# A decoder block on one core: the first norm's conditioning worked in by two weight chunks at every second output tile

## The chip, the cores and the metric

The kernel runs on one core of a Trainium2 chip. A core has five engines that work side by side, each in the order in which its own instructions stand: TensorE for matmuls (PE in the profile, PEld for its weight loads), VectorE (DVE), ScalarE (ACT), GpSimd (POOL) and SyncE (SP), which here issues the loads of weights. Sixteen DMA engines move data between the HBM and the on-chip memory. The metric is the device time of one execution in microseconds.

## The reference

The reference is one step of a decoder block (one layer, width 2048) over 288 tokens: 256 of a prompt and 8 samples of 4 tokens. The two request groups share all weights. Cut to what matters here:

```
mod = silu(c) @ w_ada + b_ada                  # 2048 -> 6 parts of 2048
sh1, sc1, g1, sh2, sc2, g2 = split(mod, 6)     # one row per sequence: 1 + 8
h    = rmsnorm(x, norm1) * (1 + sc1) + sh1     # the first norm, conditioned
proj = h @ w_in                                # pooling, gate, x/B/C, dt columns
...                                            # pooling mixer, Mamba-2 scan
x = x + g1 * (mix @ w_out)
h2 = rmsnorm(x, norm2) * (1 + sc2) + sh2
x = x + g2 * (conv_ffn(h2))                    # up, causal conv, SiLU, down
y = rmsnorm(x, norm_f)
```

"Conditioning of the first norm" is the making of `sh1` and `sc1`: 9 rows of `silu(c)` (padded to 32) times a weight matrix of 2048 × 4096. Only when they are there for some 128 rows of the hidden width can these rows of `h` be made, and only then can the projection `h @ w_in` use them.

## The kernel before, in words

Activations lie transposed: the hidden width on the 128 partitions, in 16 blocks called K tiles, and the 288 tokens along the free dimension. A projection's output tile is 128 output columns by 288 tokens. Operands of the projections are split into a high and a low part, so that each K tile of an output tile takes three matmuls: high by high, high by low, low by high (`mm3`, L221 to L223).

All weights come as chunks of 128 × 1024 words of 4 bytes (512 KB) through one set of eight buffers (`raw`), loaded by `load` (L209) on SP's queue. A chunk of the projection is then split: ScalarE casts it to the high part (L215) and VectorE subtracts to get the low part (L216); high and low have two buffers each, so a new chunk is split when the one before the last has been used up. The raw buffer is free after the subtraction. A chunk of the conditioning's weights isn't split: TensorE reads it straight from its raw buffer as float32 (`ada_mm`, L250), four narrow matmuls side by side in four column strips of the array, and the buffer is free when they are done.

The input projection begins before the conditioning of all rows is there. The K tiles are cut into six groups of 1, 1, 2, 4, 4 and 4 (`KGROUPS`). For each group in turn, `xbc_units` goes over 28 output tiles (`ET`), multiplies the group's K tiles into each, and adds the result to sums in the on-chip memory: by ScalarE's copies for the first group, by VectorE's adds (L536) for the others. While it does so, the conditioning of the next group is worked in between the output tiles: `ada_group_units` is a generator that loads one chunk, yields, and at its next step multiplies that chunk and loads another. The loop calls it once after each output tile, from tile `NX[gi]` on:

```
for i, m in enumerate(xbc_units(gi)):
    if not last:
        if i >= NX[gi]:
            next(nxt, None)
        if i == ET - 4:
            drain(nxt)
            modulate(...)
```

A step of this kind between two output tiles is called a visit here. The second group's conditioning has 4 chunks, the third's 8 (of 16 narrow passes on TensorE each, over 128 columns), and the fourth's, fifth's and sixth's 16 each (8 passes over 256 columns). A group's projection weights come in chunks of 8 output tiles for the first two groups, of 4 for the third, of 2 for the others. When the last chunk is in, the result is copied out of PSUM, transposed on TensorE and added to the bias; then `modulate` makes the group's rows of `h` (in halves again, `h1h` and `h1l`, L348 and L349).

The program text is not yet the order on the engines. A planner of the kernel language puts each engine's instructions, SP's loads too, in order when the kernel is built: it takes the earliest in the text among those that are ready by its own estimate of times, and gives out buffers as by that estimate they come free. Where it reckons a chunk late, it lets other matmuls go first; so a visit can be cut in two, or two visits can meet.

After the projection, `ada_part_units` makes the other four parts of the conditioning in the same manner; it handles two K tiles to a visit already (`AY`). Then follow the mixer, the output projection, and the feed-forward part with the gate, value and down matmuls, which fill the time from about 500 us on.

Of the kernel before, what the change touches and what calls it, by code (L numbers as in the profile page):

```python
# [19 lines left out]
KT = D // P  # L20
# [19 lines left out]
SPLIT1, SPLIT2 = 2, 2  # L40
YK = 2
NX = (10, 1, 1, 1, 1)
AY = 2

RA1, RA2, RB1, RB2, RB3 = 0.5, 0.4, 1.0, 1.0, 1.0
# [42 lines left out]
def _halves(nk):  # L88
    return [(0, 8), (8, nk - 8)]
# [40 lines left out]
def kernel(ctx: ExitStack, tc, ins, outs):  # L130
# [9 lines left out]
    def aux(name):  # L140
        return px.tile([P, 512], F32, tag="aux", name=name)
# [18 lines left out]
    ada = kp.tile([P, 6, KT, NC9], F32, name="ada")  # L160
# [8 lines left out]
    def warm_pe(n, rhs=None):  # L169

        for _ in range(n):
            nc.tensor.matmul(wps[:, :P], ones, ones if rhs is None else rhs, start=True, stop=True)
# [33 lines left out]
    def load(key):  # L206
        off, cols = S.items[key]
        t = wp[0].tile([P, RAWC], F32, tag="raw", name="raw_" + "_".join(map(str, key)))
        nc.sync.dma_start(t[:, :cols], wflat[off:off + P * cols].rearrange("(p n) -> p n", p=P))  # L209
        return t  # L210

    def split(raw, a, n, name):
        hi = wp[0].tile([P, RAWC], F32R, tag="whi", name="whi_" + name)
        lo = wp[0].tile([P, RAWC], F32R, tag="wlo", name="wlo_" + name)
        nc.scalar.copy(hi[:, :n], raw[:, a:a + n])  # L215
        nc.vector.tensor_tensor(lo[:, :n], raw[:, a:a + n], hi[:, :n].bitcast(F32), ALU.subtract)  # L216
        return hi, lo

    def mm3(ps, whi, wlo, c, bh, bl, first, last, n=P):
        w = slice(c * n, c * n + n)  # L220
        nc.tensor.matmul(ps, whi[:, w], bh, start=first, stop=False)  # L221
        nc.tensor.matmul(ps, whi[:, w], bl, start=False, stop=False)  # L222
        nc.tensor.matmul(ps, wlo[:, w], bh, start=False, stop=last)  # L223
# [23 lines left out]
    def ada_mm(ps, raw, k, c0, nb, js):  # L247
        for j in js:
            c = c0 + (j - js[0]) * nb
            nc.tensor.matmul(ps[32 * j:32 * j + 32, :nb], sc_c[:, k, :], raw[:, c:c + nb],  # L250
                             start=(k == 0), stop=(k == KT - 1), tile_position=(0, 32 * j))

    def ada_sb(ps, nb, name, r=P):
        asb = kp.tile([P, 512], F32, tag="asb", name="asb_" + name)
        nc.scalar.copy(asb[0:r, :nb], ps[0:r, :nb])
        return asb

    def ada_tr(asb, nb, name, r=P):
        pt = aux("adat_" + name)
        for i in range(nb // P):  # L260
            nc.tensor.transpose(pt[:, i * r:(i + 1) * r], asb[0:r, i * P:(i + 1) * P], ident[0:r, 0:r])
        return pt

    def ada_scale(which, part, norm, k0, gk):
        nc.vector.scalar_tensor_tensor(
            out=amul[:, which, k0:k0 + gk, :], in0=ada[:, part, k0:k0 + gk, :], scalar=1.0,
            in1=norm[:, k0:k0 + gk].unsqueeze(2).to_broadcast([P, gk, NC9]),
            op0=ALU.add, op1=ALU.mult)

    def ada_group_units(gi):  # L270

        k0, gk = KGROUPS[gi]
        nj = min(2 * gk, 4)
        nb = 2 * gk * P // nj
        per = RAWC // (nj * nb)
        ps = pa.tile([P, 512], F32, tag="ada", name=f"adag{gi}")
        for q in range(KT // per):
            raw = load(("ada", gi, q))
            yield
            if gk == 1:  # L280

                for kk in range(0, per, 2):
                    k = q * per + kk
                    for j in range(4):
                        nc.tensor.matmul(ps[32 * j:32 * j + 32, :nb], sc_c[:, k + j // 2, :],
                                         raw[:, kk * 256 + j * P:kk * 256 + j * P + P],
                                         start=(k == 0), stop=(k == KT - 2), tile_position=(0, 32 * j))
                if gi == 0 and q < WU[3]:
                    warm_pe(WU[2], raw[:, 0:P])
                continue  # L290
            for kk in range(per):
                ada_mm(ps, raw, q * per + kk, kk * nj * nb, nb, range(nj))
        r = 32 * nj
        if gk == 1:
            asb = ada_sb(ps, nb, f"g{gi}")
            pt = aux(f"adat_g{gi}")
            nc.tensor.matmul(pt[:, :r], asb[:, :nb], early[:, K_S2:K_S2 + r], start=True, stop=True)
            if gi == 0:
                warm_pe(WU[4], asb[:, 0:P])
        else:  # L300
            pt = ada_tr(ada_sb(ps, nb, f"g{gi}", r), nb, f"g{gi}", r)
        for i in range(nb // P):

            o = ada[:, 0:2, k0:k0 + gk, :].rearrange("p a (b i) c -> p a b i c", b=nj // 2)[:, :, :, i, :]
            b = bada[:, 0:2, k0:k0 + gk].rearrange("p a (b i) -> p a b i", b=nj // 2)[:, :, :, i]
            src = pt[:, i * r:(i + 1) * r].rearrange("p (a b c) -> p a b c", a=2, b=nj // 2)[:, :, :, 0:NC9]
            nc.vector.tensor_tensor(o, src, b.unsqueeze(3).to_broadcast([P, 2, nj // 2, NC9]), ALU.add)
        ada_scale(0, 1, early[:, V_N1:V_N1 + KT], k0, gk)

    def ada_part_units(part, ay=1):  # L310
        ps = pa.tile([P, 512], F32, tag="ada", name=f"adap{part}")
        for k in range(KT):
            raws = [load(("adap", part, k, h)) for h in range(2)]
            for h in range(2):
                ada_mm(ps, raws[h], k, 0, 512, range(2 * h, 2 * h + 2))
            if k % ay == ay - 1:
                yield
        asb = ada_sb(ps, 512, f"p{part}")
        yield
        pt = ada_tr(asb, 512, f"p{part}")  # L320
        for i in range(4):
            o = ada[:, part].rearrange("p (j i) c -> p j i c", j=4)[:, :, i, :]
            b = bada[:, part].rearrange("p (j i) -> p j i", j=4)[:, :, i]
            src = pt[:, i * P:(i + 1) * P].rearrange("p (j c) -> p j c", j=4)[:, :, 0:NC9]
            nc.vector.tensor_tensor(o, src, b.unsqueeze(2).to_broadcast([P, 4, NC9]), ALU.add)
        if part == 4:
            ada_scale(1, 4, vec[:, V_N2:V_N2 + KT], 0, KT)
        yield
# [54 lines left out]
    def xav(k0, gk):  # L383
        return xa[k0 // 4][:, k0 % 4:k0 % 4 + gk, :]
# [154 lines left out]
    def drain(gen):  # L539
        for _ in gen:  # L540
            pass
# [260 lines left out]
    def chain(*gens):  # L802
        for gn in gens:
            yield from gn

    adas = chain(*(ada_part_units(p, AY) for p in (2, 3, 4)))
    drain(ada_group_units(0))
    modulate(xav(0, KGROUPS[0][1]), rstd1p, 0, 0, 0, KGROUPS[0][1], "g0")
    conv0 = conv_group(0)
# [35 lines left out]
    def pull(gn, rate):  # L845

        credit[id(gn)] = credit.get(id(gn), 0.0) + rate
        while credit[id(gn)] >= 1:
            credit[id(gn)] -= 1
            next(gn, None)  # L850

    for gi in range(len(KGROUPS)):
        last = gi + 1 == len(KGROUPS)
        if last:
            hi, lo = split(load(("dt",)), 0, KT * NH, "dt")
            ps = pm.tile([P, 512], F32, tag="mm", name="mm_dt")
            for k in range(KT):
                mm3(ps[0:NH, :N], hi, lo, k, xhi[0][k], xlo[0][k], k == 0, k == KT - 1, NH)
            dt_stage(ps)
        else:  # L860
            if gi == 1:
                nc.sync.dma_start(vec, ins["vec"])
            if gi == 4:
                late_loads()
            nxt = ada_group_units(gi + 1)
            k0, gk = KGROUPS[gi + 1]
        for i, m in enumerate(xbc_units(gi)):
            if not last:
                if i >= NX[gi]:
                    next(nxt, None)  # L870
                if i == ET - 4:
                    drain(nxt)
                    modulate(xav(k0, gk), rstd1, 0, 0, k0, gk, f"g{gi + 1}")
            else:
                pull(back, 0.5 if m < 20 else RB1) if m >= 9 else None
                pull(adas, RA1 / AY)

# [3 lines left out]
    for m in list(range(4 + 3 * ZEARLY, 16)) + ULATE:  # L881
        for _ in uz_units(m):
            n += 1
            for gn in late.values():
                pull(gn, 0.5)
            pull(adas, RA2 / AY)
            pull(back, RB2 if n <= zlast else RB3)
# [3 lines left out]
        if m < 4:  # L891
            late[m] = pool_units(m)
            next(late[m])
    pull(adas, TA / AY)
    for h, (_, n) in enumerate(_halves(KT)):
# [69 lines left out]
    for m in range(16):  # L965
# [9 lines left out]
        squares(m, "a")  # L975
        pull(adas, (1 + (m >= 14 - ADA_OUT)) / AY)
        if m == 13:
# [300 lines left out]
```

## Time and profile before

| | |
|---|---|
| median of 3 runs | 1402.48 us (1401.91 to 1403.09) |
| the profiled execution | 1403.24 us, of which the span of the profile is 1401.5 us |
| TensorE busy | 99% of the span |
| VectorE, ScalarE, GpSimd busy | 59%, 41%, 20% |
| read from HBM | 309.71 MB, 228 GB/s over the span |
| granted clock of TensorE, mean | 0.997 |

The profile shows one execution. Busy times are of instructions; on TensorE the matmuls are pipelined, so that several are in flight at once and their shown durations (some 0.3 us) overlap; the distance between starts tells the rate. In the timeline a line is a start in us from the span's begin, a duration in us, the engine, the line of the kernel, the operation, what it writes and reads, and how many instructions the line stands for; in brackets stands the idle time before it and what ended it. A float32 matmul of the conditioning is shown as two passes. The names: `raw_ada` is a chunk of the conditioning's weights, `adag` its sums, `raw_xbc`, `whi_xbc` and `wlo_xbc` a chunk of the projection's and its two parts, `xbc` the projection's sums, `cvp` and `cvs` where they are added up.

### The profile page before, as it was taken

How to read it: one execution, taken by the hardware profiler on the slowest of the kernel's cores; microseconds unless marked ns; L12 is line 12 of the kernel's file. 1: busy time of each engine (PE TensorE's matmuls, PEld its weight loads, DVE VectorE, ACT ScalarE, POOL GpSimd, SP SyncE). 2: the span in 40 equal slices, each digit the busy share in tenths (PEclk: the TensorE clock that was granted, in tenths of full speed). 3: DMA queues.
4: the chain of work that ended last, by engine and by line, in shares of the span. 5: the costliest groups of instructions: out<-in, count | busy, mean ns of one | idle time of the engine just before them, and what ended most of it. 6: DMA issues, size and time to landing. Idle time of an engine off the chain costs nothing.

```text
span 1401.5 us, 26531 instructions
## 1 busy us (share of the span) xinstructions
PE 1383.4 (99%) x10589; PEld 1260.6 (90%) x10589; DVE 829.3 (59%) x1429; ACT 578.4 (41%) x941; POOL 276.7 (20%) x490
## 2 busy tenths in 40 slices
PE   8999999998999999999999999999999999999998
PEld 6677887776668898989999999999999999999998
DVE  3775667867555436844666445666665466666553
ACT  5322324365573333533443333434443344444443
POOL 0000003554332212311211000212220011122121
PEclk9999999999999999999999999999999999999999
DMA  8889886867779886688655555655555555555531
GB/s 335 320 316 321 293 286 232 331 252 254 290 259 358 311 327 245 208 277 289 231 191 177 161 169 179 206 188 187 177 181 170 178 194 188 188 193 197 181 117 68
DMA packets 97195, 323.14 MB, mean 231 GB/s; under 512 B 10736, under 2 KB 19888, under 8 KB 97072
## 3 DMA queue, kind: packets, MB, share of 16 engines
q1 hardware_dynamic: 93168, 310.57, 63.1%
q0 software_dynamic: 3184, 9.69, 2.0%
q8 instruction: 83, 1.36, 0.4%
q10 hardware_dynamic: 720, 1.19, 0.2%
q14 instruction: 40, 0.33, 0.1%
HBM read 309.71 MB, written 10.39 MB: 228 GB/s over the span
## 4 chain that ended last, share of the span: by engine, by line
PE 70%; DVE 1%; issue 0%; ACT 0%; POOL 0%; DVEq 0%; POOLq 0%; ACTq 0%
PE mm_down L223 7%; PE mm_down L221 7%; PE mm_down L222 7%; PE mm_gate L223 6%; PE mm_gate L221 6%; PE mm_val L222 6%; PE mm_gate L222 6%; PE mm_val L223 6%; PE mm_val L221 6%; PE mm_out L221 2%; PE mm_out L222 2%; PE mm_out L223 2%; PE adap L250 2%; PE mm_up L221 1%; PE mm_up L222 1%; PE mm_up L223 1%
## 5 line engine op out<-in xcount | busy, mean ns | idle before, releaser
L221 PE MATMUL mm_down<-ah,whi_down 128*128 128x288 f32 x688 | 203.7, 296 | 0.0
L223 PE MATMUL mm_down<-ah,wlo_down 128*128 128x288 f32 x688 | 203.5, 296 | 0.0
L222 PE MATMUL mm_down<-al,whi_down 128*128 128x288 f32 x688 | 203.3, 295 | 0.0
L223 PE MATMUL mm_gate<-h2h,wlo_gate 128*128 128x288 f32 x640 | 190.2, 297 | 0.0
L221 PE MATMUL mm_gate<-h2h,whi_gate 128*128 128x288 f32 x640 | 189.8, 297 | 0.0
L222 PE MATMUL mm_gate<-h2l,whi_gate 128*128 128x288 f32 x640 | 189.3, 296 | 0.0
L222 PE MATMUL mm_val<-h2l,whi_val 128*128 128x288 f32 x640 | 188.8, 295 | 0.0
L223 PE MATMUL mm_val<-h2h,wlo_val 128*128 128x288 f32 x640 | 188.5, 294 | 0.0
L221 PE MATMUL mm_val<-h2h,whi_val 128*128 128x288 f32 x640 | 188.0, 294 | 0.0
L216 DVE TENSOR_TENSOR wlo_gate<-raw_gate,whi_gate 128x1024 fp32r<-128x1024 f32 x80 | 98.0, 1225 | 141.1 <-ACT whi_gate L215 141.0
L216 DVE TENSOR_TENSOR wlo_down<-raw_down,whi_down 128x1024 fp32r<-128x1024 f32 x96 | 108.1, 1126 | 115.6 <-ACT whi_down L215 114.7
L215 ACT CAST whi_down<-raw_down 128x1024 fp32r<-128x1024 f32 x96 | 92.2, 961 | 168.6 <-PE mm_down L222 121.9
L215 ACT CAST whi_gate<-raw_gate 128x1024 fp32r<-128x1024 f32 x80 | 83.9, 1050 | 169.2 <-PE mm_gate L222 73.2
L221 PE MATMUL xbc<-h1h,whi_xbc 128*128 128x288 f32 x448 | 139.2, 313 | 1.5 <-ACT h1h L348 1.3
L215 ACT CAST whi_val<-raw_val 128x1024 fp32r<-128x1024 f32 x80 | 84.1, 1051 | 127.3 <-issue 102.4
L222 PE MATMUL xbc<-h1l,whi_xbc 128*128 128x288 f32 x448 | 132.1, 296 | 0.0
L223 PE MATMUL xbc<-h1h,wlo_xbc 128*128 128x288 f32 x448 | 130.5, 298 | 0.9 <-DVE wlo_xbc L216 0.9
L222 PEld LDWEIGHTS mm_down<-al,whi_down 128*128 128x128 f32 x688 | 129.7, 189 | 0.0
L223 PEld LDWEIGHTS mm_down<-ah,wlo_down 128*128 128x128 f32 x688 | 129.6, 188 | 0.0
L221 PEld LDWEIGHTS mm_down<-ah,whi_down 128*128 128x128 f32 x688 | 129.6, 188 | 0.0
L221 PEld LDWEIGHTS mm_gate<-h2h,whi_gate 128*128 128x128 f32 x640 | 120.5, 188 | 5.0 <-ACT ah L1031 4.2
L222 PEld LDWEIGHTS mm_gate<-h2l,whi_gate 128*128 128x128 f32 x640 | 120.7, 189 | 0.0
(341 smaller groups left out, 3100.8 us busy)
## 6 DMA issues: line engine op xcount, KB each, us to landing
raw_adap<-wflat SPq DMA_DIRECT2D x128, 512.0 KB, 5.1
raw_gate<-wflat SPq DMA_DIRECT2D x80, 512.0 KB, 3.6
raw_val<-wflat SPq DMA_DIRECT2D x80, 512.0 KB, 3.5
raw_ada<-wflat SPq DMA_DIRECT2D x64, 512.0 KB, 5.3
raw_xbc<-wflat SPq DMA_DIRECT2D x55, 512.0 KB, 5.8
raw_down<-wflat SPq DMA_DIRECT2D x48, 512.0 KB, 3.5
raw_out<-wflat SPq DMA_DIRECT2D x32, 512.0 KB, 6.5
raw_down<-wflat SPq DMA_DIRECT2D x32, 384.0 KB, 3.0
```

Source lines behind the costliest of these rows:

```text
L215: nc.scalar.copy(hi[:, :n], raw[:, a:a + n])
L216: nc.vector.tensor_tensor(lo[:, :n], raw[:, a:a + n], hi[:, :n].bitcast(F32), ALU.subtract)
L221: nc.tensor.matmul(ps, whi[:, w], bh, start=first, stop=False)
L222: nc.tensor.matmul(ps, whi[:, w], bl, start=False, stop=False)
L223: nc.tensor.matmul(ps, wlo[:, w], bh, start=False, stop=last)
L250: nc.tensor.matmul(ps[32 * j:32 * j + 32, :nb], sc_c[:, k, :], raw[:, c:c + nb], start=(k == 0), stop=(k == KT - 1), tile_position=(0, 32 ...
```

## The change

From the third K group on, the generator loads two chunks at a step and multiplies two at its next; the loop calls it at every second output tile instead of at every one. For the first two groups (`gk == 1`) all stays as it is. The number of chunks, their matmuls and their order among themselves are the same. For the third group the last chunk is multiplied at the visit after tile 9, for the later groups after tile 17, as before; the rest that `drain` would take at tile `ET - 4` is empty in both.

```diff
+AG = 2
 AY = 2
...
         ps = pa.tile([P, 512], F32, tag="ada", name=f"adag{gi}")
-        for q in range(KT // per):
-            raw = load(("ada", gi, q))
+        at = 1 if gk == 1 else AG
+        for q0 in range(0, KT // per, at):
+            raws = [load(("ada", gi, q)) for q in range(q0, q0 + at)]
             yield
-            if gk == 1:
+            for q, raw in zip(range(q0, q0 + at), raws):
+                if gk > 1:
+                    for kk in range(per):
+                        ada_mm(ps, raw, q * per + kk, kk * nj * nb, nb, range(nj))
+                    continue
                 for kk in range(0, per, 2):
...
-                continue
-            for kk in range(per):
-                ada_mm(ps, raw, q * per + kk, kk * nj * nb, nb, range(nj))
...
         for i, m in enumerate(xbc_units(gi)):
             if not last:
-                if i >= NX[gi]:
+                if i >= NX[gi] and (gk == 1 or (i - NX[gi]) % AG == 0):
                     next(nxt, None)
```

## The prediction

> **What bounds the kernel now.** I read the page first (busy shares, slices), then the table of waits, then windows of the stage that the change touches, then the timeline of single visits. The page and the waits of TensorE:
>
> ```profile
> PE 1383.4 (99%) x10589; PEld 1260.6 (90%) x10589; DVE 829.3 (59%) x1429; ACT 578.4 (41%) x941; POOL 276.7 (20%) x490
> ...
> PE   8999999998999999999999999999999999999998
> ...
> PEclk9999999999999999999999999999999999999999
> ...
> PE mm_uz L223 <- DVE wlo_uz L216: 3.0, 1, 3.0
> ...
> PE xbc L221 <- ACT h1h L348: 1.3, 1, 1.3
> ...
> PE xbc L223 <- DVE wlo_xbc L216: 0.9, 3, 0.5
> ```
>
> TensorE is occupied for 99% of the span, at the full granted clock in every slice, and its longest wait in the whole run is 3.0 us. In the stage in question, some 37 to 193 us, it waits for next to nothing: the two xbc rows. So a microsecond less of TensorE work there is a microsecond off the end, unless something else becomes late. What could become late are the weights; the windows say how near that is (columns: busy us of each engine and instructions, granted clock, share of the DMA engines, GB/s):
>
> ```profile
> 10.00:16.00 6.00, 5.70 (x59) 3.92 (x59) 1.99 (x3) 0.70 (x2) 0.00 (x0) 1.00 1.03 420
> ...
> 49.00:87.00 38.00, 37.83 (x294) 26.17 (x295) 27.57 (x83) 8.38 (x11) 0.60 (x2) 1.00 0.89 324
> 107.00:136.00 29.00, 29.00 (x253) 21.78 (x251) 13.60 (x32) 6.61 (x7) 0.00 (x0) 1.00 0.92 311
> 157.00:193.00 36.00, 36.00 (x312) 27.06 (x310) 17.20 (x39) 7.64 (x8) 0.00 (x0) 1.00 0.94 325
> ```
>
> TensorE is full in all of them, but the DMA engines are 89 to 94% busy too: a second resource lies close behind the first. Where the queue is long (10 to 16 us) they move 420 GB/s.
>
> **The price of a visit.** A visit is a switch of TensorE from the projection's matmuls to the conditioning's narrow ones and back. The timeline of TensorE around a visit with one chunk (x8: four matmuls, each shown as two passes) and around one in which two chunks happen to meet (x16):
>
> ```profile
> 111.95 0.29 PE L223 MATMUL xbc<-h1h,wlo_xbc 128*128 128x288 f32 x1
> 112.17 0.64 PE L250 MATMUL adag<-raw_ada,sc_c 128*32 128x256 f32 x8
> 112.74 0.40 PE L221 MATMUL xbc<-h1h,whi_xbc 128*128 128x288 f32 x1
> 112.98 0.30 PE L222 MATMUL xbc<-h1l,whi_xbc 128*128 128x288 f32 x1
> 113.11 0.29 PE L223 MATMUL xbc<-h1h,wlo_xbc 128*128 128x288 f32 x1
> ...
> 82.46 0.30 PE L223 MATMUL xbc<-h1h,wlo_xbc 128*128 128x288 f32 x1
> 82.70 1.07 PE L250 MATMUL adag<-raw_ada,sc_c 128*32 128x256 f32 x16
> 83.70 0.40 PE L221 MATMUL xbc<-h1h,whi_xbc 128*128 128x288 f32 x1
> 83.93 0.30 PE L222 MATMUL xbc<-h1l,whi_xbc 128*128 128x288 f32 x1
> ```
>
> Matmuls are pipelined, so starts are what counts. Projection matmuls start 0.13 us apart (112.98 to 113.11). From the last one before a visit to the second one after it is 1.03 us with one chunk (111.95 to 112.98) and 1.47 us with two (82.46 to 83.93). Less the two ordinary steps (0.26) a single visit costs 0.77 us and a double one 1.21 us. Two singles are 1.54, so each pair that is merged saves 0.33 us.
>
> **How many pairs.** Before, the sixth group's conditioning has a visit after every tile, and so has the fifth's from 107 us on; the fourth's and the third's are not laid out as the program is written:
>
> ```profile
> 157.41 0.64 PE L250 MATMUL adag<-raw_ada,sc_c 128*32 128x256 f32 x8
> ...
> 159.77 0.64 PE L250 MATMUL adag<-raw_ada,sc_c 128*32 128x256 f32 x8
> ...
> 192.72 0.64 PE L250 MATMUL adag<-raw_ada,sc_c 128*32 128x256 f32 x8
> ...
> 107.47 0.64 PE L250 MATMUL adag<-raw_ada,sc_c 128*32 128x256 f32 x8
> ...
> 135.71 0.64 PE L250 MATMUL adag<-raw_ada,sc_c 128*32 128x256 f32 x8
> ...
> 52.41 0.62 PE L250 MATMUL adag<-raw_ada,sc_c 128*32 128x256 f32 x2
> ...
> 53.42 0.63 PE L250 MATMUL adag<-raw_ada,sc_c 128*32 128x256 f32 x6
> ...
> 84.56 0.64 PE L250 MATMUL adag<-raw_ada,sc_c 128*32 128x256 f32 x8
> ...
> 37.68 0.84 PE L250 MATMUL adag<-raw_ada,sc_c 128*32 128x128 f32 x18
> ...
> 42.13 0.64 PE L250 MATMUL adag<-raw_ada,sc_c 128*32 128x128 f32 x16
> ...
> 45.63 1.08 PE L250 MATMUL adag<-raw_ada,sc_c 128*32 128x128 f32 x32
> ```
>
> The sixth group: (192.72 − 157.41) / 2.36 + 1 = 16 visits. The fifth: 13 from 107.47 to 135.71 and three stretches ahead of them. The fourth (from 52.41 to 84.56): 19 stretches for 16 chunks, since the planner cut visits in two where it reckoned a chunk late. The third (from 37.68): 8 stretches for 8 chunks, one of them already a pair.
>
> **The sum, edit by edit.**
> - Fifth and sixth group: 16 visits each become 8. 16 × 0.33 = −5.3 us.
> - Third group: 8 visits become 4, −1.3 us by the same price: a second chunk lengthens a visit there by 0.44 (1.08 for x32, 0.64 for x16; a chunk is x16 here), in the rows above by 0.43 (1.07, 0.64).
> - Fourth group: the planner, not the program, cuts the visits there, and it would go on doing so. If all 19 become 8 it is −3.6 us; if nothing merges it is 0. I take 0, since the x2 and x6 rows show a split that the edit doesn't address.
> - The transposes and the adds that end a group come after the visit at tile 17, before and after (for the third group, tile 9). Nothing of the modulation moves in the program.
> - Loads. Every chunk is still loaded once from SP, 64 in all; the order on SP changes. A chunk's load moves ahead of one projection load, and the first chunk of each pair stays in its buffer one tile longer. Both shorten the lead of the projection's weights, which I price now. The queues of POOL and ACT issue nothing that is moved.
>
> Buffers are eight for all weights. Call X(c) the projection's load for tiles 2c and 2c+1 in the fifth group's tiles. Before, 3c − 1 loads stand ahead of X(c), so 3c − 8 buffers must have come free; that is reached at the visit after tile 2c − 6. After, 3c loads stand ahead and 3c − 7 must be free; that is reached at the double visit after tile 2c − 5. The timelines of SP, ACT, DVE and TensorE, and how long the projection's loads took to land between 150 and 200 us:
>
> ```profile
> 160.47 1.94 SPq L209 DMA_DIRECT2D raw_ada<-wflat  x2
> ...
> 162.82 0.33 SPq L209 DMA_DIRECT2D raw_xbc<-wflat  x1
> ...
> 167.53 0.33 SPq L209 DMA_DIRECT2D raw_xbc<-wflat  x1
> ...
> 169.16 1.05 ACT L215 CAST whi_xbc<-raw_xbc 128x1024 fp32r<-128x1024 f32 x1 [3.66 <-PE xbc L222]
> 174.28 1.05 ACT L215 CAST whi_xbc<-raw_xbc 128x1024 fp32r<-128x1024 f32 x1 [4.08 <-DMA raw_xbc<-wflat]
> ...
> 176.35 0.42 DVE L536 TENSOR_TENSOR cvp<-cvp,xbc 128x256 f32<-128x256 f32 x1 [1.83 <-PE xbc L223]
> 176.78 1.22 DVE L216 TENSOR_TENSOR wlo_xbc<-raw_xbc,whi_xbc 128x1024 fp32r<-128x1024 f32 x1
> ...
> 179.16 0.40 PE L221 MATMUL xbc<-h1h,whi_xbc 128*128 128x288 f32 x1
> ...
> 179.53 0.29 PE L223 MATMUL xbc<-h1h,wlo_xbc 128*128 128x288 f32 x1
> ...
> DMA to landing us min/median/max: 3.4/5.1/6.7
> ```
>
> X(6) is issued at 167.53 and first used at 179.16: a lead of 11.6 us, and its cast at 174.28 already waits for the landing. After, the lead is four tiles and two double visits: 4 × 12 × 0.13 + 2 × 1.21 = 8.7 us. What must fit into it: landing (5.1 median, 6.7 longest), cast 1.05, subtraction 1.22, of which 0.37 lies behind the first use: 7.0 us at the median, 8.6 at the longest, 9.0 when an add sits ahead of the subtraction (0.43, from 176.35 to 176.78). So it fits by 1.7 us or misses by 0.3. TensorE is what waits then, and behind it the next visit, whose buffers SP waits for. I take 0.3 us for the last three projection loads in each of two groups, some 1.8 us; the ends are 0 and, if the miss of 0.3 doubles because a late weight also frees its buffer late, 0.6 us for all 16 pairs, 9.6 us.
>
> The sum: −5.3 − 1.3 + 1.8 = −4.8 us; 0.3 of it I give up for a changed order in the fourth group, −4.5 us. The profiled execution took 1403.24 us (span 1401.5 and 1.7 around it), so 1398.7 on that footing; the median of the runs, 1402.48, is 0.76 lower: 1398.0. Later stages are bounded by TensorE, so they move up as a whole. From no change a measurement of this kernel can tell about 0.2%, 2.8 us.
>
> **A ceiling on the DMA rate.** A pair of tiles with two chunks moves three loads of 524 KB (128 × 1024 words), 1.57 MB, in 2 × 2.36 = 4.71 us, 334 GB/s; after, in 4.38 us, 359 GB/s. The 10 to 16 us window moved 420, so the rows allow it. [...] The observed 325 at 94% busy would be 346 GB/s when full, 4.55 us a pair, a gain of 0.16 instead of 0.33: 16 × 0.16 = 2.6 us; chunks that landed well ahead (the load is issued up to eight buffers early) cover part of it.
>
> **Rivals.**
> - *Lateness eats it.* The rate above or the lead holds each pair near 4.55 us; with nothing from the third group the time is 1403.2 − 2.6, on the median 1399.9, and with some stalls up to 1405. For it: DMA busy at 94%, the cast at 174.28 waiting for a landing. Against: only late casts, no TensorE wait on weights over 0.5 us now.
> - *Slower: the buffers.* Holding two chunks until one visit leaves X(c) late by more than it saves. It decides from a lead of 8.7 us being less than landing, cast, add and subtraction plus the 0.33 saved. With the longest landing 9.0 is needed, a miss of 0.3, and the late free of X(c − 2) feeds it back two or three times over: 16 × 0.6 − 5.3 = +4 to 16 × 0.9 − 5.3 = +9, 1407 to 1412. Against: the median landing leaves 1.7 us.
> - *It merges more.* The planner joins the fourth group's visits too, and hides the lead: 59 stretches become 28, 31 × 0.33 = −10.2: 1392.3.
> - *It doesn't merge.* The planner puts chunks where it reckons them landed, as at 52.41, and cuts the pairs again: no change, 1402.5, or some 4 more switches a group.
>
> **Numbers.** Forecast (gain of 3 to 8 us, 1394 to 1399.6): 0.52. More than that: 0.11. Lateness or no merging, within 0.2%: 0.19. Slower by over 0.2%: 0.18. Faster 0.63. The range leaves out a tenth on either side or a little less: 1392.5, short of the full merge, to 1405.5, where the buffer rival begins.
>
> **What would show it.** In the profile after: L250 in stretches of x16 at every second tile between about 100 and 190 us; two tiles and a visit taking 4.38 us; TensorE waits on whi_xbc and wlo_xbc (L215, L216) of no more than 2 us in all; casts of whi_xbc ended by the DMA in more cases. Wrong would be: x8 stretches as before, or waits on wlo_xbc of 0.5 us and more at every second tile.

## The result, and the profile after

The changed kernel is slower: 1409.99 us in the median of four runs (1408.77 to 1412.38) against 1402.59 us (1401.91 to 1403.09) for the kernel before on the same chip, a ratio of 1.0055 with a 95% interval of 1.0039 to 1.0071. The profiled execution took 1408.77 us (span 1407.0 us), 5.5 us more than that of before; it is the fastest of the four.

Line numbers of the changed kernel stand one higher up to the adds (the cast is L216, the subtraction L217, the conditioning's matmuls L251); the adds are L541. The same rows of the page as before, and the waits of TensorE from 30 to 220 us:

```profile
PE 1384.5 (98%) x10589; PEld 1264.4 (90%) x10589; DVE 828.8 (59%) x1429; ACT 578.4 (41%) x941; POOL 276.8 (20%) x490
...
PE   8999999998999999999999999999999999999998
...
PEclk9999999998999999999999999999999999999999
```

```profile
PE xbc L224 <- DVE wlo_xbc L217: 2.4, 3, 1.6
PE xbc L222 <- DVE cvs L541: 1.4, 2, 1.0
PE xbc L222 <- ACT whi_xbc L216: 1.3, 3, 0.6
PE adat_g L262 <- ACT asb_g L256: 0.9, 2, 0.5
```

The page hardly differs (the 8 in the clock's row stands for a stretch near 320 us, long after the part that was changed). The waits do: where TensorE waited 0.7 us by the same view before, it now waits 6.0 us, for both parts of the projection's weights, for the adds, and for the copy that ends a group of the conditioning. A table by stage says where. A stage is the time from the first projection matmul of one K group to that of the next (from the timeline of TensorE); in it the next group's conditioning is worked in. The stage of the fifth group's tiles ends where the matmuls of the dt columns begin, which stand ahead of the sixth group's.

| output tiles of | conditioning worked in | before, us | after, us | difference |
|---|---|---|---|---|
| second group (from 38.95; after 38.30) | third group | 23.53 | 27.95 | +4.42 |
| third group | fourth group | 34.47 | 35.66 | +1.19 |
| fourth group | fifth group | 55.61 | 56.04 | +0.43 |
| fifth group | sixth group | 57.00 | 56.37 | −0.63 |
| the rest, to the end | | 1191.90 | 1192.68 | +0.78 |

With a start 0.65 us earlier these make up the 5.5 us. So most of the loss is not where the prediction looked for it (in the conditioning of the fifth and sixth group, where −3.5 us were forecast) but at the start of the changed part. Windows over it, after:

```profile
37.00:49.00 12.00, 10.74 (x163) 8.23 (x162) 6.97 (x23) 2.64 (x7) 1.21 (x2) 1.00 0.89 299
49.00:87.00 38.00, 36.50 (x272) 25.49 (x275) 26.00 (x76) 6.52 (x8) 0.63 (x1) 0.96 0.80 283
```

In the second row TensorE lacks 1.50 us, and its granted clock is 0.96 where it was 1.00. Both come from one place. First before, the timelines of SP, ACT and DVE around the second chunk of the projection's weights for the second group's tiles (call it X1) and the last of the third group's conditioning (A7):

```profile
38.38 0.33 SPq L209 DMA_DIRECT2D raw_xbc<-wflat  x1
39.06 0.33 SPq L209 DMA_DIRECT2D raw_ada<-wflat  x1
...
42.84 1.05 ACT L215 CAST whi_xbc<-raw_xbc 128x1024 fp32r<-128x1024 f32 x1 [3.29 <-DMA raw_xbc<-wflat]
48.21 0.27 ACT L255 COPY asb_g<-adag 128x128 f32<-128x128 f32 x1 [4.32 <-PE adag L250]
...
46.17 1.22 DVE L216 TENSOR_TENSOR wlo_xbc<-raw_xbc,whi_xbc 128x1024 fp32r<-128x1024 f32 x1
...
49.37 0.19 DVE L307 TENSOR_TENSOR ada<-adat_g,early 128x36 f32<-128x36 f32 x1
```

X1 is loaded, then A7. X1 is cast as soon as it lands (42.84) and subtracted at 46.17; the group's copy (48.21) and bias add (49.37) come behind. After, the two loads have changed places, and the timelines of SP, PE, ACT and DVE, with the time X1's load took to land, read:

```profile
37.73 0.33 SPq L210 DMA_DIRECT2D raw_ada<-wflat  x1
38.42 5.48 SPq L210 DMA_DIRECT2D raw_xbc<-wflat  x4
...
44.40 1.95 PE L251 MATMUL adag<-raw_ada,sc_c 128*32 128x128 f32 x64
46.79 0.33 PE L262 MATMUL adat_g<-early,asb_g 128*128 128x128 f32 x1 [0.44 <-ACT asb_g L256]
47.74 0.40 PE L222 MATMUL xbc<-h1h,whi_xbc 128*128 128x288 f32 x1 [0.61 <-ACT whi_xbc L216]
...
49.53 0.66 PE L224 MATMUL xbc<-h1h,wlo_xbc 128*128 128x288 f32 x3 [0.72 <-DVE wlo_xbc L217]
51.16 0.37 PE L222 MATMUL xbc<-h1h,whi_xbc 128*128 128x288 f32 x1 [0.97 <-DVE cvs L541]
...
46.47 0.27 ACT L256 COPY asb_g<-adag 128x128 f32<-128x128 f32 x1 [7.58 <-PE adag L251]
46.64 1.05 ACT L216 CAST whi_xbc<-raw_xbc 128x1024 fp32r<-128x1024 f32 x1
...
47.60 0.73 DVE L345 TENSOR_SCALAR h_g<-h_g,amul,ada 128x256 f32<-128x256 f32 x2
48.26 1.22 DVE L217 TENSOR_TENSOR wlo_xbc<-raw_xbc,whi_xbc 128x1024 fp32r<-128x1024 f32 x1
...
DMA to landing us min/median/max: 5.2/5.2/5.2
```

X1, issued at 38.42, is there at 43.6. But on ScalarE the planner has put the group's copy ahead of X1's cast, and the copy needs all of the group's matmuls: ScalarE stands idle for 7.58 us with X1 in its buffer and casts it at 46.64, 3 us after it landed. On VectorE the bias add and the modulation have moved ahead of X1's subtraction (48.26). TensorE has by then run four chunks in one stretch (x64, 44.40) and has no projection weights left. It waits four times, 2.7 us in all.

What follows costs nearly as much again. Windows of the changed kernel, and two consecutive projection matmuls in them:

```profile
46.00:50.00 4.00, 2.22 (x26) 1.48 (x14) 2.24 (x5) 1.55 (x3) 1.84 (x2) 1.00 0.94 318
50.00:52.00 2.00, 1.03 (x8) 0.87 (x7) 1.87 (x8) 1.38 (x3) 0.00 (x0) 0.97 0.94 377
52.00:54.00 2.00, 2.00 (x10) 2.00 (x10) 1.50 (x7) 0.00 (x0) 0.00 (x0) 0.50 0.97 387
54.00:56.00 2.00, 2.00 (x8) 0.81 (x7) 1.80 (x5) 0.62 (x1) 0.00 (x0) 0.68 0.37 150
```

```profile
53.16 0.44 PE L223 MATMUL xbc<-h1l,whi_xbc 128*128 128x288 f32 x1
53.40 0.44 PE L224 MATMUL xbc<-h1h,wlo_xbc 128*128 128x288 f32 x1
```

From 46 to 52 us TensorE is busy for 3.25 of 6 us. Then its granted clock falls to 0.50: projection matmuls start 0.24 us apart (53.16 to 53.40) instead of 0.13. The time lost to it is 0.03 × 2 + 0.50 × 2 + 0.32 × 2 = 1.7 us, as much as 3.4 us at half the clock. Idle time (2.75 us, where the same six us of before had some 0.2) and clock together are 4.3 of the 4.4 us that this stage lost.

Among the third group's tiles the same two kinds of load have changed places. Before, the fifth chunk of the projection's weights for these tiles (call it Y5) is loaded at 75.90 us and the last chunk of the fourth group's conditioning at 77.48; after, that last chunk goes first (80.45) and Y5 behind it (80.89). The timelines of ACT and DVE after:

```profile
87.72 0.37 ACT L256 COPY asb_g<-adag 128x256 f32<-128x256 f32 x1 [9.56 <-PE adag L251]
...
90.43 1.21 DVE L217 TENSOR_TENSOR wlo_xbc<-raw_xbc,whi_xbc 128x1024 fp32r<-128x1024 f32 x1
```

The subtraction stands behind the modulation (from 89.18) again, and TensorE waits 3.0 us in this stage (0.5 before), 1.55 us of it for that subtraction; the clock stays at 1.00 here. Y5 also lands only at 87.28, so two things delay it; no run moves this load alone. The stage lost more than the table's 1.19 us: two chunks of the fifth group's conditioning (2 × 0.44 = 0.9 us by the prediction's price) now fall into the next stage, so that 2.1 us belong here, and the next stage gained 0.5 instead of losing 0.4.

In the sixth group the pairs are there, but not all of them. TensorE's visits after:

```profile
164.38 1.07 PE L251 MATMUL adag<-raw_ada,sc_c 128*32 128x256 f32 x16
168.76 1.07 PE L251 MATMUL adag<-raw_ada,sc_c 128*32 128x256 f32 x16
...
184.05 0.29 PE L223 MATMUL xbc<-h1l,whi_xbc 128*128 128x288 f32 x1
184.27 0.62 PE L251 MATMUL adag<-raw_ada,sc_c 128*32 128x256 f32 x2
184.82 0.40 PE L224 MATMUL xbc<-h1h,wlo_xbc 128*128 128x288 f32 x1
185.06 0.30 PE L222 MATMUL xbc<-h1h,whi_xbc 128*128 128x288 f32 x1
```

Whole pairs stand 4.38 us apart, the figure of the prediction. From the sixth pair on the planner has cut them: the order of TensorE's instructions has stretches of 8, 8, 8, 8, 8, 1, 7, 5, 4, 7 narrow matmuls, ten instead of eight, and in the fifth group 1, 4, 3, 8, 8, 8, 8, 8, 1, 7, 5, 3. A stretch of a single matmul (x2 in the profile) costs as much as one of four: 1.01 us from 184.05 to 185.06, against 1.03 for x8 before.

### The profile page after: what moved, and what is told of

The parts are those of the page before. It is cut to its first block, busy times and chain, and to the rows that moved or that the text cites. A ratio compares the mean times of both kernels' runs of the same rounds, so it can differ in the third digit from the quotient of the medians.

```text
span 1407.0 us, 26532 instructions
## 1 busy us (share of the span) xinstructions
PE 1384.5 (98%) x10589; PEld 1264.4 (90%) x10589; DVE 828.8 (59%) x1429; ACT 578.4 (41%) x941; POOL 276.8 (20%) x490
## 3 DMA queue, kind: packets, MB, share of 16 engines
q10 hardware_dynamic: 720, 1.19, 0.2%
## 4 chain that ended last, share of the span: by engine, by line
PE 69%; DVE 1%; issue 0%; ACT 0%; POOL 0%; DVEq 0%; POOLq 0%; ACTq 0%
PE mm_down L222 7%; PE mm_down L224 7%; PE mm_down L223 6%; PE mm_gate L224 6%; PE mm_gate L222 6%; PE mm_val L223 6%; PE mm_gate L223 6%; PE mm_val L224 6%; PE mm_val L222 6%; PE mm_out L222 2%; PE mm_out L223 2%; PE mm_out L224 2%; PE adap L251 2%; PE mm_up L222 1%; PE mm_up L223 1%; PE mm_up L224 1%
## 5 line engine op out<-in xcount | busy, mean ns | idle before, releaser
L217 DVE TENSOR_TENSOR wlo_gate<-raw_gate,whi_gate 128x1024 fp32r<-128x1024 f32 x80 | 98.6, 1233 | 141.9 <-ACT whi_gate L216 141.4
L217 DVE TENSOR_TENSOR wlo_down<-raw_down,whi_down 128x1024 fp32r<-128x1024 f32 x96 | 108.2, 1127 | 116.0 <-ACT whi_down L216 115.2
L216 ACT CAST whi_down<-raw_down 128x1024 fp32r<-128x1024 f32 x96 | 92.3, 961 | 168.8 <-PE mm_down L223 120.3
L216 ACT CAST whi_gate<-raw_gate 128x1024 fp32r<-128x1024 f32 x80 | 83.9, 1050 | 169.3 <-PE mm_gate L223 73.7
L216 ACT CAST whi_val<-raw_val 128x1024 fp32r<-128x1024 f32 x80 | 84.1, 1051 | 126.4 <-issue 102.5
```

## The experiments

The edits are shown against the kernel that the text names. `gi` counts from 0, so 2 is the third group. The last column gives the stages of the profiled execution, as in the table above. Each ratio is to runs of the kernel before on the same chip, whose median was 1402.47 to 1402.92 us in the experiments.

| run | time, us | ratio to before (95%) | tiles of 2nd, 3rd, 4th, 5th group, us |
|---|---|---|---|
| before | 1402.59 | | 23.53, 34.47, 55.61, 57.00 |
| the change | 1409.99 | 1.0055 (1.0039 to 1.0071) | 27.95, 35.66, 56.04, 56.37 |
| pairs in 5th and 6th only | 1401.31 | 0.999 (0.998 to 0.9999) | 23.53, 34.47, 55.91, 55.81 |
| pairs in 3rd only | 1406.55 | 1.0024 (1.0015 to 1.0034) | 26.45, 34.76, 55.61, 57.01 |
| pairs in 4th only | 1405.31 | 1.0016 (1.0007 to 1.0026) | 22.90, 37.59, 57.00, 57.01 |
| matmuls in pairs in all four, loads as before | 1397.29 | 0.996 (0.9945 to 0.9975) | 23.40, 33.90, 53.52, 54.24 |
| loads in pairs, matmuls as before | 1413.53 | 1.0077 (1.0062 to 1.0092) | 28.09, 36.38, 58.39, 58.39 |
| one load swapped | 1408.18 | 1.0034 (1.0021 to 1.0048) | 26.83, 34.76, 55.61, 57.01 |
| 3rd only, that load put back | 1403.30 | 1.0000 (0.999 to 1.0009) | 23.77, 34.47, 55.61, 57.01 |
| 3rd only, copy on VectorE | 1406.72 | 1.0025 (1.0015 to 1.0034) | 26.53, 34.76, 55.61, 57.01 |
| the change, nine buffers | 1406.96 | 1.0027 (1.0017 to 1.0036) | 29.09, 35.66, 56.04, 54.24 |
| before, nine buffers | 1402.51 | 0.9996 (0.9987 to 1.0006) | 23.54, 34.47, 55.60, 57.00 |
| matmuls in pairs, 5th and 6th only | 1398.02 | 0.9961 (0.9947 to 0.9975) | 23.53, 34.47, 53.51, 54.24 |
| matmuls in pairs in 3rd and 4th, in fours in 5th and 6th | 1400.41 | 0.9984 (0.9975 to 0.9994) | 23.41, 34.02, 54.72, 55.49 |

The theory after the result: merging matmuls gains what was forecast; moving the loads loses more, early, through one swapped load. The rivals: that two chunks are held until one visit and the eight buffers run short, that the longer visits do the harm, and that ScalarE's order alone is the trouble.

**Which group loses.** Three runs make the change in some groups only, against the changed kernel (the first; the others have `(2,)` and `(3,)`):

```diff
-        at = 1 if gk == 1 else AG
+        at = AG if gi in (4, 5) else 1
...
-                if i >= NX[gi] and (gk == 1 or (i - NX[gi]) % AG == 0):
+                if i >= NX[gi] and (gi + 1 not in (4, 5) or (i - NX[gi]) % AG == 0):
```

> Pairs (loads and matmuls) for the fifth and sixth group's conditioning alone; the third and fourth as before. Theory A (the loss is made among the second and third group's tiles, by what loading two conditioning chunks ahead of the projection's weights does to the order there; the later groups gain): 2 us faster than before, about 1400.5, with 13 and 10 stretches of the conditioning instead of 16 and 16. Rival B (the loss is the eight buffers: holding two chunks makes the projection's weights late, most of all in the later groups): slower than before, 1404 to 1407, with waits on wlo_xbc at every second tile.

> Pairs for the third group's conditioning alone. Theory A: most of the loss, 3.5 to 5 us over before, about 1406.5, since in the changed kernel the second group's tiles took 4.4 us longer (27.95 against 23.53). Rival B: no more than 1 us, since this group has 8 of the 56 chunks.

> Pairs for the fourth group's conditioning alone. Theory A: 1 to 3 us over before, about 1404.5 (in the changed kernel the third group's tiles took 1.2 us longer, and a part of the tiles before them). Rival B: 1 us either way.

Measured: 1401.31, 1406.55 and 1405.31 us. The fifth and sixth group gain a little (1.5 us, where 2 were expected), the third and the fourth each lose, as expected. With pairs in the third group alone the second group's tiles take 2.9 us more; with pairs in the fourth alone the third's take 3.1 us more, again with a fall of the clock:

```profile
80.00:84.00 4.00, 3.01 (x39) 1.61 (x37) 1.43 (x7) 1.32 (x2) 0.00 (x0) 1.00 1.01 394
84.00:88.00 4.00, 2.45 (x12) 2.22 (x13) 3.79 (x7) 2.38 (x5) 0.99 (x2) 0.71 1.02 391
88.00:92.00 4.00, 4.00 (x18) 4.00 (x18) 2.41 (x10) 0.88 (x1) 0.00 (x0) 0.50 0.86 324
92.00:96.00 4.00, 4.00 (x26) 3.42 (x26) 3.40 (x9) 1.20 (x2) 0.00 (x0) 0.94 0.18 47
```

Those are windows of the run with pairs in the fourth group: 2.5 us idle, and 0.29 × 4 + 0.50 × 4 + 0.06 × 4 = 3.4 us lost to the clock, where the same stage of before had 0.5 us of waits. Four visits fewer (13 to 9) and two chunks that now fall into the next stage take 4 × 0.33 + 2 × 0.44 = 2.2 us off again, which leaves the 3.1. The three runs' differences (−1.5, +3.7, +2.5 us against some 1402.8) add up to 4.7 us, not to the 7.4 of the whole; they aren't independent, and how much the clock takes differs from run to run (the profiled execution with pairs in the fourth group is the slowest of ten and has one more stretch of half clock, some 3.4 us from 246 us).

The run with pairs in the fifth and sixth alone also shows the lead that the prediction worked out, in the timelines of SP, ACT and PE and the landing times of the projection's loads from 150 to 200 us:

```profile
168.56 1.53 SPq L210 DMA_DIRECT2D raw_xbc<-wflat  x1
...
176.57 1.05 ACT L216 CAST whi_xbc<-raw_xbc 128x1024 fp32r<-128x1024 f32 x1 [4.76 <-DMA raw_xbc<-wflat]
...
177.67 0.40 PE L222 MATMUL xbc<-h1h,whi_xbc 128*128 128x288 f32 x1 [0.36 <-ACT whi_xbc L216]
...
DMA to landing us min/median/max: 4.5/6.3/7.9
```

From issue to first use are 9.1 us, with 0.36 us of waiting in it; the landing took up to 7.9 us where it took 6.7 before. That is TensorE's only wait in this stretch.

**Loads and matmuls apart.** One run loads one chunk per tile, as before, but multiplies two at every second tile; the other loads two at every second tile and multiplies one per tile. Against the changed kernel, first the one and then the other:

```diff
-            raws = [load(("ada", gi, q)) for q in range(q0, q0 + at)]
-            yield
+            raws = []
+            for q in range(q0, q0 + at):
+                raws.append(load(("ada", gi, q)))
+                yield
...
-                if i >= NX[gi] and (gk == 1 or (i - NX[gi]) % AG == 0):
+                if i >= NX[gi]:
```

```diff
             for q, raw in zip(range(q0, q0 + at), raws):
                 if gk > 1:
+                    if q > q0:
+                        yield
...
-                if i >= NX[gi] and (gk == 1 or (i - NX[gi]) % AG == 0):
+                if i >= NX[gi]:
```

> All four groups: matmuls in pairs at every second tile, but one load at every tile, so that the loads stand as before. Theory A in its strict form (it is the order of the loads alone): the loss goes, and 16 pairs of the last two groups gain 0.33 each: 5 us faster than before, about 1397. If it is the merged visits that do the harm among the second group's tiles: still some 2 us lost there, about 1400. Rival B: as slow as the changed kernel, 1407 to 1410, since the buffers are held as long.

> All four groups: loads in pairs at every second tile as in the changed kernel, but one chunk multiplied at every tile. Theory A (the loads' order does the harm, the merged visits the gain): slower than the changed kernel, which still has the gain of some 12 merged pairs: 1410 to 1414. Rival C: as before, 1402 to 1404.

Measured: 1397.29 us and 1413.53 us, both as expected. The first beats both kernels. Its visits in the sixth group (first and last of eight, all x16) and its waits of TensorE from 30 to 220 us:

```profile
156.01 1.07 PE L251 MATMUL adag<-raw_ada,sc_c 128*32 128x256 f32 x16
...
186.63 1.07 PE L251 MATMUL adag<-raw_ada,sc_c 128*32 128x256 f32 x16
```

```profile
PE xbc L224 <- DVE wlo_xbc L217: 0.5, 1, 0.5
PE xbc L222 <- DVE cvs L543: 0.2, 1, 0.2
```

Eight whole pairs save 57.00 − 54.24 = 2.76 us, 0.345 each; the waits are those of before. The first chunk of a pair is held in its buffer for two tiles here as well, so holding that one isn't what costs; in the changed kernel both are held so long. The second run has all of the early loss and none of the gain: in the sixth group it has 18 visits where there were 16, and its stages over the fourth and fifth group's tiles are 2.8 (0.9 of it the two chunks that moved) and 1.4 us longer than before, without a wait of TensorE there.

**One load.** The kernel before, with only A7's load moved ahead of X1, and the kernel with pairs in the third group alone, with that load put back behind X1:

```diff
+        kept = []
...
-            raw = load(("ada", gi, q))
+            raw = kept.pop() if kept else load(("ada", gi, q))
+            if gi == 2 and q == 6:
+                kept.append(load(("ada", gi, 7)))
```

```diff
-            raws = [load(("ada", gi, q)) for q in range(q0, q0 + at)]
+            raws = [load(("ada", gi, q)) for q in range(q0, q0 + at - (at > 1 and q0 == 6))]
             yield
+            if at > 1 and q0 == 6:
+                raws.append(load(("ada", gi, 7)))
+                yield
...
-                if i >= NX[gi] and (gi + 1 not in (2,) or (i - NX[gi]) % AG == 0):
+                if i >= NX[gi] and (gi + 1 not in (2,) or (i - NX[gi]) % AG == 0 or i == 8):
```

> The kernel before with one change: the third group's last conditioning chunk is loaded one tile earlier, so that on SP it stands ahead of the projection's second chunk of weights instead of behind it. No visit is merged by the program. Theory A (one swapped load is enough: the copy of the conditioning's sums then stands ahead of the cast of the projection's chunk on ScalarE, and the second group's tiles wait for it): 2.5 to 4 us slower than before, about 1406, with the second group's tiles at 26 to 27 us (23.53 before). Rival C (it is the longer visits, not the swap): no slower than 1 us.

> Pairs for the third group alone as in the run of that kind, but its last chunk's load again behind the projection's second chunk. Theory A: the loss of 3.7 us goes, within 1 us of before, 1402.5. Rival C: still 3 us slower, since the visits are as long as there (its last two visits are x48 and x16 instead of x64).

Measured: 1408.18 us and 1403.30 us. One swap of two 512 KB loads in the kernel before makes the second group's tiles 3.3 us longer; taking it back brings the kernel with pairs in the third group to a ratio of 1.0000, with visits of x48 and x16, so the longer visits aren't the cause. The stage of the swap is as expected (26.83 us), but its median, 5.4 us over before, is more than the 2.5 to 4 expected. The profiled execution is the fastest of the five (1405.98 us); the mean granted clock of the others goes from its 0.996 down to 0.992, so some of the rest is the clock. ScalarE and TensorE in the run with the one swap:

```profile
46.73 0.27 ACT L255 COPY asb_g<-adag 128x128 f32<-128x128 f32 x1 [7.71 <-PE adag L250]
46.89 1.05 ACT L215 CAST whi_xbc<-raw_xbc 128x1024 fp32r<-128x1024 f32 x1
...
47.99 0.40 PE L221 MATMUL xbc<-h1h,whi_xbc 128*128 128x288 f32 x1 [0.62 <-ACT whi_xbc L215]
```

The same order and, to 0.01 us, the same four waits of TensorE as in the changed kernel (0.44, 0.62, 0.73 and 0.98 us), without a single merged pair in the program.

**ScalarE alone?** Pairs in the third group only, with the group's copy on VectorE, so that nothing stands ahead of X1's cast:

```diff
-        nc.scalar.copy(asb[0:r, :nb], ps[0:r, :nb])
+        (nc.vector.tensor_copy if name == "g2" else nc.scalar.copy)(asb[0:r, :nb], ps[0:r, :nb])
```

> Pairs for the third group alone, with its loads in the changed order, but the sums of the conditioning are copied out of PSUM by VectorE instead of ScalarE, so that on ScalarE nothing stands ahead of the cast of the projection's chunk. Theory A with ScalarE's order as the way: the cast begins at the landing, about 43.7 us instead of 46.6, and 2 us or more of the 3.7 are back, 1403 to 1404.5. If the late landing of the chunk itself is the way: still 1406.

Measured: 1406.72 us, no better than with the copy on ScalarE (1406.55), against the expectation of the theory with ScalarE alone; the number is that of the rival, the late landing. ACT, DVE and PE:

```profile
44.80 1.05 ACT L216 CAST whi_xbc<-raw_xbc 128x1024 fp32r<-128x1024 f32 x1 [5.39 <-DMA raw_xbc<-wflat]
...
48.09 0.74 DVE L345 TENSOR_SCALAR h_g<-h_g,amul,ada 128x256 f32<-128x256 f32 x2
48.74 1.22 DVE L217 TENSOR_TENSOR wlo_xbc<-raw_xbc,whi_xbc 128x1024 fp32r<-128x1024 f32 x1
...
50.01 0.66 PE L224 MATMUL xbc<-h1h,wlo_xbc 128*128 128x288 f32 x3 [1.60 <-DVE wlo_xbc L217]
```

The cast is early again, as soon as X1 lands, but the subtraction is not: it stands behind the modulation on VectorE. The late landing isn't what holds it: the cast ends at 45.85, and before, the subtraction began at 46.17 and did no harm; here VectorE stands idle from 45.57 to 46.93, until the copy that comes first in its order can run, and takes X1 at 48.74. The copy on ScalarE isn't the cause by itself; the whole end of the group has passed X1, on both engines.

**Buffers.** Nine buffers instead of eight (a tile of the mixer, `s2`, shares the place of another), with the change and without it:

```diff
-RAW1, RAW2 = 8, 1
+RAW1, RAW2 = 9, 1
...
-        s2 = mx.tile([P, G6], F32, tag="s2", name=f"s2_{g}")
+        s2 = mx.tile([P, G6], F32, tag="yo", name=f"s2_{g}")
```

> The whole change, with nine weight buffers in place of eight (room is made by letting the mixer's s2 share the place of yo). Theory A (the early loss is the swapped load, and the cut pairs of the sixth group are the want of a buffer): the second group's tiles stay at 27 to 28 us, the sixth group's conditioning comes in eight whole pairs and the stage over the fifth group's tiles takes 54.2 to 54.8 us in place of 56.4; the time is 1407.5 to 1408.5. Rival (buffers cause the whole loss): the second group's tiles come back to 23.5 and the time to 1400 or less.

> The kernel before with the same nine buffers, the control of the run beside it. Both theories: 1402 to 1403, stages within 0.3 us of before, since no TensorE wait on weights was over 0.5 us there. If the ninth buffer helps or hurts by itself, it shows here.

Measured: 1406.96 us and 1402.51 us. The ninth buffer does nothing for the kernel before. With the change it makes the sixth group's conditioning eight whole pairs and brings the stage from 56.37 to 54.24 us: the cuts there were the want of a buffer. The fifth group stays cut in the same places (56.04) and the early loss stays: 29.09 us for the second group's tiles, where 27 to 28 were expected, and 1.1 more than in the changed kernel with the same order of work. In this execution the clock stayed at half for some 6.8 us (0.91 from 48 to 52 us, 0.50 from 52 to 56, 0.74 from 56 to 60). The time is 0.5 us under the range expected.

**What a visit costs.** Two edits of the run with matmuls in pairs and one load per tile: pairs for the fifth and sixth group alone, and fours for these two while the third and fourth keep their pairs:

```diff
-        at = 1 if gk == 1 else AG
+        at = AG if gi >= 4 else 1
```

```diff
-        at = 1 if gk == 1 else AG
+        at = 1 if gk == 1 else AG if gi < 4 else 4
```

> One load per tile as before, and matmuls in pairs for the fifth and the sixth group alone. By the price of 0.33 us a merged pair: the sixth group 8 pairs, 2.7 us off the stage over the fifth group's tiles (57.0 to 54.3); the fifth 14 stretches to 8 to 10, 1.5 to 2 us; 1398.3 in all, against 1397.3 with the third and fourth group too. If the merged pairs of the earlier groups carry more than 1 us, this run is above 1399.

> As the run with one load per tile and matmuls in pairs (1397.29 us), but four chunks to a visit for the fifth and the sixth group, one load per tile still. In the planned order the fifth group comes in 11 stretches (of 1, 8, 3, 4, 16, 1, 8, 7, 5, 7, 4 narrow matmuls), the sixth in 8 (16, 16, 9, 7, 4, 4, 4, 4). Theory C (a visit costs 0.33 us once and 0.44 us for every begun set of four narrow matmuls, since four run side by side): the fifth group 11 x 0.33 + 19 x 0.44 = 12.0 us against 10 x 0.33 + 17 x 0.44 = 10.8 with pairs, the sixth 10.1 against 9.7: 1.6 us more in all, the stages over the fourth's and the fifth's tiles some 54.7 us each, 1398.9 in all. Rival (only the number of visits counts): 0.33 us more, 1397.6, the stage over the fifth's tiles 54.2.

Measured: 1398.02 us and 1400.41 us. The first splits the gain of 1397.29: the fifth and sixth group give 2.10 and 2.76 us by their stages, 4.9 in all, the third and fourth 0.7. The run in fours is 1.5 us over its expectation and 2.8 over that of its rival, which counts visits alone. The stage over the fourth group's tiles is 54.72 us, as expected from 0.33 per visit and 0.44 per begun set of four narrow matmuls. The fifth's is 55.49, 0.8 more than expected, most of it one late chunk: at 171 us two projection matmuls start 0.79 us apart, 0.66 more than their step, and the second had waited for its low part.

## Why the prediction was wrong

The forecast was −4.5 us and the profiled execution gives +5.5. Of the 10 us between them, 5.7 are the term of the third group, 2.4 those of the fifth and sixth (gain and lateness together) and 1.8 the fourth's with the 0.3 given up for it, the two chunks that moved put back to where they were. Point by point, by its own steps:

- *The price of a visit* was right: 0.33 forecast, 0.345 measured over eight whole pairs. It was incomplete: 0.44 belongs to a begun set of four narrow matmuls, not to a chunk, so a pair that is cut into 1 and 7 pays three sets and not two. With both prices the sixth group of the changed kernel (10 stretches, 18 sets) comes to 10 × 0.33 + 18 × 0.44 = 11.2 us against 16 × 0.77 = 12.3, a gain of 1.1, less 0.4 of waits: 0.7, measured 0.63.
- *Fifth and sixth group, −5.3*: measured +0.43 (−0.45 without the two chunks that moved there) and −0.63. The term took whole pairs for granted in these groups and allowed for cuts in the fourth alone. The rival "it doesn't merge" named the mechanism, with too little weight. With the loads as before the term is nearly right: −4.9, with eight whole pairs in the sixth group and ten stretches in the fifth.
- *Third group, −1.3, and fourth, 0*: here the prediction failed. Measured +4.4 and +1.2 in the profiled execution, the latter 2.1 with the two chunks that moved on. The step is the edit "Loads": "A chunk's load moves ahead of one projection load". It was priced as a shorter lead, in the fifth and sixth group only. In the third group the one moved load changes the planned order of ScalarE and VectorE: the end of the group and its modulation go ahead of the split of the projection's chunk. "Nothing of the modulation moves in the program" was true of the program and false of the engines. That one load does it is shown by moving it alone, for the third group; for the fourth the same order is seen and not tested alone. The gain of 1.3 us wasn't there either: with matmuls in pairs and the loads as before, the second group's tiles take 23.40 us, 0.1 less than before, in seven stretches instead of eight.
- *Lead and lateness, +1.8*: the lead was 8.7 us by the forecast and 9.1 in the run with pairs there; landing took up to 7.9 us, longer than the 6.7 assumed, yet TensorE waited only 0.4 us once in that run, and 0.4 in two waits in the changed kernel. As a wait, the term was too large. But against the run with pairs in these groups and loads as before (53.51 and 54.24 us), loading in pairs cost the two stages 1.7 (56.04, less the 0.9 that moved there) and 2.1 us (56.37), nearly all of it as cut visits, as at 184.27, where one narrow matmul stands ahead of the first matmul with a low part.
- *The rate*: in the run with matmuls in pairs the eight pairs of the sixth group stand (186.63 − 156.01) / 7 = 4.37 us apart, so no ceiling held them. Whether one would in a longer stretch is open: the window from 156 to 186.6 us moved 329 GB/s there, less than the 360 that three loads of 524 KB in 4.37 us would need, so some chunks had landed ahead.
- *The slower rival* had the sign and even the size (1407 to 1412) but not the mechanism: it put the loss on held buffers in the later groups. Those cost 2.1 us in the sixth group (the ninth buffer), by cutting pairs and not by waits for weights; the loss proper is an order on the engines' queues, shown for the third group and seen in the fourth. That the time lies in this rival's range is luck.
- *"At the full granted clock in every slice"* was read from slices of 35 us, in which 1.7 us lost is 5% and the digit stays at 9. It wasn't so even before: from 318.67 to 325.50 us the granted clock was 0.50, and over 300 to 350 us 0.93. Of the two xbc rows beside it only 0.5 us lies between 30 and 220 us, so TensorE waited even less there than the prediction says.

That the forecast of 1398.0 us is nearly the time of the run with matmuls in pairs in the fifth and sixth group (1398.02) is partly luck. Of the terms of its sum, that run has only the −5.3, and gives −4.9; it has neither the gain in the third group nor the lateness.

The 0.78 us of the rest aren't the change's own as far as the traces go. Near 320 us, where both kernels have waits of TensorE (the longest 3.0 us in each), the clock is at 0.50 for 10.24 us after (321.53 to 331.77) and for 6.83 before; the mean from 300 to 350 us is 0.90 and 0.93, and 0.90 too in the kernel before with nine buffers. Half of the 3.41 us between 10.24 and 6.83 is 1.7, more than the difference.

What stays open: why the planner prefers the group's end once A7 is loaded first (its own estimates are in no trace); why the fifth group's pairs stay cut with nine buffers; and what makes the spread of the changed kernel's runs (3.6 us). All four have a mean clock of 0.995 to three digits, and 0.001 of the run is 1.4 us, so the clock is at most a part of it.

## What to carry to other kernels

Merging small matmuls and merging their loads are two edits; make the first without the second, and leave the order of loads on the queue as it was. When a load passes another one, compare the order on every engine that works on either, above all where a group's last chunk is involved, because all that waits for that chunk may pass with it. And price a wait of TensorE with what the clock took after it: here 1.7 us after 2.7 us of waits from 46 to 52 us, and nothing after the 3.0 us among the third group's tiles.

## What was not expected of the hardware

The clock: after six us in which TensorE was busy for a little over half of the time (3.25 us from 46 to 52 us in the changed kernel, with no single wait over 1.0 us), it ran at 0.50 for 3.4 us, there (51.88 to 55.29) and in the runs with pairs in the third group alone, with one load swapped, with the copy on VectorE and with loads in pairs; in the run with pairs in the fourth group (busy for 2.05 of the four us from 82 to 86), and in the changed kernel with nine buffers, for twice that, some 6.8 us. In the changed kernel 2.7 us of waits and 1.7 us lost to the clock so make 4.4 us; with nine buffers the second group's tiles lost 5.6 (29.09 against 23.53). It isn't certain: in the changed kernel a like stretch from 87 to 94 us (4.06 of 7 us busy) left the clock at 1.00.

What makes it fall is not shown. TensorE worked in every microsecond from 46 to 52 us (the least, 0.19 us, from 50 to 51). The busy share alone doesn't decide it: TensorE was busy for 1.71 of the 3.41 us before the fall (48.47 to 51.88), and in the like stretch for 1.35 of as long a time (88.50 to 91.91) without a fall. And in the run with pairs in the fourth group the clock fell once, at 246 us (0.76 from 244 to 248 us, 0.81 from 248 to 252), with TensorE busy for 3.98 of the four us from 240 to 244 and for all of the next four. How long it stays at half differs too: 3.41 and 10.24 us (321.53 to 331.77) in the changed kernel, 6.83 us (318.67 to 325.50) in the kernel before.

The narrow matmuls: four in the four column strips take as long as one (1.03 us and 1.01 us for the visit), so a stretch costs by the set of four that it begins.
